# A two-layer encoder trunk in float32: the feed-forward's first projection by Strassen's seven products, tokens in two halves

## The chip, the cores and the metric

One Trainium2 chip, one core. The metric is the device time of one execution in microseconds (us), the median of several runs. The engines are named as the profile names them: PE (TensorE, matrix products), PEld (its weight loads), DVE (VectorE), ACT (ScalarE), POOL (GpSimd), SP (SyncE, which issues most DMA transfers). SBUF is the on-chip memory that all engines read, PSUM the banks that PE writes its sums to.

## What is computed

Two groups of tokens (272 and 1040 with the 16 meta tokens) pass through two layers of width 1024. Layer 0 mixes with a state-space scan and a gated recurrence, layer 1 with windowed attention; after each mixer comes the same gated feed-forward, on which the change works:

```python
def conv_ffn(h, w_up, conv_w, conv_b, w_down):      # w_up 1024 x 5632, w_down 2816 x 1024
    u = dwconv(h @ w_up, conv_w, conv_b, 1)          # width-3 depthwise convolution over tokens
    a, g = u[..., :2816], u[..., 2816:]
    return (gelu(g) * a) @ w_down

for layer in range(2):
    h = h + mixer(rmsnorm(h, norm_mix_g[layer]))
    h = h + conv_ffn(rmsnorm(h, norm_ffn_g[layer]), w_up[layer], ...)
h = rmsnorm(h, final_norm_g)
```

All of it is float32. PE multiplies in the format float32r; a product of two float32 matrices is made of three passes over a high part (the rounded value) and a low part (the rest): high x high, high x low, low x high.

## The kernel before, in words

Activations lie feature-major: 1024 features are 8 blocks of 128 partitions, and the 1316 columns are the tokens with pads. `hh` and `hl` (8 x 1316) hold the high and low parts of the normalized activations, `h` the residual, all in SBUF through the whole feed-forward.

`unit` (L233 to L243) brings in a weight unit of 128 x 1024 floats: a DMA on SP's queue, the high part by a cast on ACT (L241), the low part by a subtraction on DVE (L242), or on POOL where the caller asks for it, which only attention's projections do. `mm3_steps` (L251 to L261) issues the three passes: L256, L257 and L261.

`ffn` (from L320) takes the 22 blocks of 128 features of each half of `w_up` two at a time. For each block and each of three chunks of 438 tokens (440 columns with the neighbours that the convolution needs) `conv` makes 8 x 3 = 24 matmuls into one PSUM bank (tags a and b in turn), and the convolution on ACT (L337) and DVE (L339, L341), both straight out of PSUM. `gate` adds the gelu (ACT L347), the product with a (DVE L348), and the split into high and low parts (ACT L351, DVE L352). Then the two blocks of `w_down` are multiplied, chunk by chunk, 8 output blocks of 6 matmuls, into banks c and d, and DVE adds each to `h` (L384):

```python
for f in fs:
    ua = up_unit(f)
    a = [conv(f, c, *ua, "a") for c in range(NCH)]
    ug = up_unit(NF + f)
    for c in range(NCH):
        acts[f, c] = gate(f, c, a[c], ug)
downs = [self.unit(wd[f * 128:(f + 1) * 128, :], b=1024) for f in fs]
for c in range(NCH):
    for m in range(KD):
        ps = self.bank("cd")
        self.mm3(ps[:, :CH], [(downs[j][0][:, m * 128:(m + 1) * 128], ...) for j, f in enumerate(fs)])
        nc.vector.tensor_tensor(out=hs, in0=hs, in1=ps[:, :CH], op=ALU.add)
```

Per layer that is 44 x 3 x 24 = 3168 matmuls of 440 columns for the first projection and 11 x 3 x 8 x 6 = 1584 of 438 columns for the second. The weights are read once per layer.

`project_out` (L1247 to L1292) multiplies a mixer's output by its 1024 x 1024 matrix in three thirds of the tokens, 192 matmuls of about 438 columns each; in layer 1 the first third is done beside attention (`out_block`, L1202). `norm` (L265) makes the RMSNorm in four steps that are placed between other work. A scheduler orders the instructions of each engine by a simulation of its own; only in attention does the program's order stand for PE.

## Time and profile before

| | us |
|---|---|
| median of 3 runs (3090.25 to 3095.92) | 3090.98 |
| span of the profiled execution | 3089.7 |
| PE busy | 2934.9 (95%) |
| DVE busy | 1854.6 (60%) |
| ACT busy | 1133.7 (37%) |
| POOL busy | 200.9 (7%) |
| feed-forward of layer 0, about | 620 to 1560 |
| attention, about | 1560 to 2050 |
| feed-forward of layer 1, about | 2080 to 3010 |

The profiled execution's own time is its span, 3089.7 us; the runs' median lies 1.3 us above it. Matmuls overlap in the records (one lasts longer than the distance to the next), so a rate is read from the starts, or from a stretch divided by its count. DVE's records overlap a little in the same way.

### The profile page before, as it was taken

What the parts mean: (1) busy time and instruction counts of PE and PEld (TensorE: products, weight loads), DVE (VectorE), ACT (ScalarE), POOL (GpSimd) and SP (SyncE); (2) the same over time, 40 slices, a digit from 0 to 9 for tenths busy, and PEclk for the clock granted to TensorE, in tenths of its full rate; (3) what the DMA queues carried; (4) which work ended last, traced back from release to release, by engine and by line L of the source; (5) the groups of instructions that cost most, each with busy time, mean ns of one, the idle gap of its engine ahead of it and who ended that gap; (6) DMA issues with size and microseconds to landing.
All of it is one profiled execution on the core that took longest, in us unless ns stands there. A gap on an engine that the chain in (4) does not pass through costs nothing.

```text
span 3089.7 us, 39910 instructions
## 1 busy us (share of the span) xinstructions
PE 2934.9 (95%) x15424; PEld 2695.8 (87%) x15424; DVE 1854.6 (60%) x3386; ACT 1133.7 (37%) x2038; POOL 200.9 (7%) x356
## 2 busy tenths in 40 slices
PE   6999667999999999999999999989999999999998
PEld 5988446999999999999988887779999999999997
DVE  8998685365545555545574777757555555545555
ACT  4445683342222222222243666634222222222222
POOL 1000000000000000000003334300000000000000
PEclk9999788999999999999999999999999999999999
DMA  5331432311111011111136667761111011111101
GB/s 145 83 93 53 109 109 93 101 41 42 41 35 36 27 41 41 41 35 41 35 109 157 140 137 167 172 187 52 55 35 36 28 40 41 41 35 41 35 28 76
DMA packets 276376, 220.55 MB, mean 71 GB/s; under 512 B 33403, under 2 KB 257627, under 8 KB 276187
## 3 DMA queue, kind: packets, MB, share of 16 engines
q1 hardware_dynamic: 233755, 169.89, 19.4%
q0 software_dynamic: 35280, 31.98, 5.2%
q10 hardware_dynamic: 7152, 16.13, 1.4%
q8 instruction: 122, 2.00, 0.3%
q14 instruction: 67, 0.55, 0.1%
HBM read 167.71 MB, written 48.14 MB: 70 GB/s over the span
## 4 chain that ended last, share of the span: by engine, by line
PE 80%; DVE 10%; DMA 3%; ACT 3%; issue 2%; SPq 1%; POOL 0%; DVEq 0%; POOLq 0%; ACTq 0%
PE ps_a L256 10%; PE ps_a L261 10%; PE ps_a L257 9%; PE ps_b L261 7%; PE ps_b L257 7%; PE ps_b L256 7%; PE ps_d L261 4%; PE ps_c L261 4%; PE ps_d L256 4%; PE ps_d L257 4%; PE ps_c L256 4%; PE ps_c L257 4%; DVE z L692 1%; PE ps_c L1056 1%; PE ps_d L1075 1%
## 5 line engine op out<-in xcount | busy, mean ns | idle before, releaser
L256 PE MATMUL ps_a<-hh,whi 128*128 128x440 f32 (+4 forms) x1824 | 659.2, 362 | 29.4 <-ACT hh L907 17.3
L257 PE MATMUL ps_a<-hl,whi 128*128 128x440 f32 (+4 forms) x1824 | 654.6, 359 | 1.0 <-DVE hl L908 0.5
L261 PE MATMUL ps_a<-hh,wlo 128*128 128x440 f32 (+4 forms) x1824 | 653.2, 358 | 0.3 <-DVE wlo L242 0.3
L257 PE MATMUL ps_b<-hl,whi 128*128 128x440 f32 (+2 forms) x1136 | 413.0, 364 | 0.0
L261 PE MATMUL ps_b<-hh,wlo 128*128 128x440 f32 (+2 forms) x1136 | 412.1, 363 | 0.0
L256 PE MATMUL ps_b<-hh,whi 128*128 128x440 f32 (+2 forms) x1136 | 412.0, 363 | 0.0
L256 PEld LDWEIGHTS ps_a<-hh,whi 128*128 128x128 f32 x1824 | 348.2, 191 | 53.6 <-ACT hh L907 18.2
L242 DVE TENSOR_TENSOR wlo<-raw,whi 128x1024 fp32r<-128x1024 f32 x176 | 213.4, 1222 | 255.3 <-ACT whi L241 204.0
L261 PEld LDWEIGHTS ps_a<-hh,wlo 128*128 128x128 f32 x1824 | 347.7, 191 | 20.8 <-issue 2.6
L241 ACT CAST whi<-raw 128x1024 fp32r<-128x1024 f32 x194 | 201.1, 1047 | 448.0 <-PE ps_d L257 198.9
L257 PEld LDWEIGHTS ps_a<-hl,whi 128*128 128x128 f32 x1824 | 347.8, 191 | 18.6 <-DVE hl L231 1.0
L384 DVE TENSOR_TENSOR h<-h,ps_c 128x438 f32<-128x438 f32 x264 | 161.0, 610 | 175.6 <-PE ps_c L261 175.4
L384 DVE TENSOR_TENSOR h<-h,ps_d 128x438 f32<-128x438 f32 x264 | 161.1, 610 | 111.6 <-PE ps_d L261 111.0
L256 PEld LDWEIGHTS ps_b<-hh,whi 128*128 128x128 f32 x1136 | 214.3, 189 | 14.3
L261 PEld LDWEIGHTS ps_b<-hh,wlo 128*128 128x128 f32 x1136 | 213.8, 188 | 14.0
L257 PEld LDWEIGHTS ps_b<-hl,whi 128*128 128x128 f32 x1136 | 213.7, 188 | 13.5
L337 ACT ACTIVATE a<-ps_a,cw 128x438 f32<-128x438 f32 x92 | 65.9, 716 | 378.8 <-PE ps_a L261 375.2
L256 PE MATMUL ps_d<-xh,whi 128*128 128x438 f32 x528 | 191.5, 363 | 0.0
L256 PE MATMUL ps_c<-xh,whi 128*128 128x438 f32 x528 | 191.4, 362 | 0.0
L257 PE MATMUL ps_c<-xl,whi 128*128 128x438 f32 x528 | 191.0, 362 | 0.0
L261 PE MATMUL ps_c<-xh,wlo 128*128 128x438 f32 x528 | 191.0, 362 | 0.0
L257 PE MATMUL ps_d<-xl,whi 128*128 128x438 f32 x528 | 190.9, 361 | 0.0
(403 smaller groups left out, 4766.6 us busy)
## 6 DMA issues: line engine op xcount, KB each, us to landing
raw<-in_w_up SPq DMA_DIRECT2D x88, 512.0 KB
raw<-in_w_down SPq DMA_DIRECT2D x44, 512.0 KB
qs<-st SPq DMA_DIRECT2D x48, 219.0 KB
q<-qs POOLq DMA_DIRECT2D x80, 128.0 KB, 3.5
raw<-in_w_o SPq DMA_DIRECT2D x20, 512.0 KB
raw<-in_w_out_ab SPq DMA_DIRECT2D x16, 512.0 KB
raw<-in_w_in_ab SPq DMA_DIRECT2D x12, 512.0 KB
raw<-in_w_qkv SPq DMA_DIRECT2D x12, 512.0 KB
```

Source lines behind the costliest of these rows:

```text
L241: nc.scalar.copy(hi, raw)
L242: (low or nc.vector).tensor_tensor(out=lo, in0=raw, in1=hi.bitcast(F32), op=ALU.subtract)
L256: yield nc.tensor.matmul(ps, ah, bh, start=(j == 0), stop=False)
L257: yield nc.tensor.matmul(ps, ah, bl, start=False, stop=False)
L261: yield nc.tensor.matmul(ps, al, bh, start=False, stop=(j == n - 1))
L337: nc.scalar.activation(out=t, in_=ps[:, 1:CH + 1], func=AF.Identity, scale=cw[:, 1, m:m + 1], bias=cw[:, 3, m:m + 1])
L384: nc.vector.tensor_tensor(out=hs, in0=hs, in1=ps[:, :CH], op=ALU.add)
L692: v.tensor_tensor_scan(out=f0[h, s0:s0 + 4 * NK][:, ::step], data0=fm[h, ::step], data1=f1[h, 1:1 + 4 * NK][:, ::step], initial=0.0, op0=A ...
L1056: nc.tensor.transpose(pt[:m, j, :n], s[:n, j, j0:j0 + m], self.ident[:n, :n])
L1075: nc.tensor.matmul(ov, vt, y[:m, :, :n], start=(x + i == 0), stop=(last and i == 1))
```

## The change

The first projection. Two blocks of output features (256 rows), the 1024 input features as two halves of 512, and two quarters of the tokens make a 2 x 2 by 2 x 2 block product: eight block products, which Strassen's algorithm (in Winograd's form) makes with seven. `pair` does them: each is 4 x 3 = 12 matmuls of 330 or 332 columns. Per layer there are 22 pairs for each half of the tokens, so 2 x 22 x 7 x 12 = 3696 matmuls.

What the seven products need is made by other engines. `part` forms four sums of weight blocks a pair (five in the first two pairs of a half), 128 x 512, on POOL. `supply` splits each product's weights (128 x 512) into high and low parts: the cast on ACT, the subtraction on POOL for five products of seven and on DVE for products 4 and 7. There are 8 such tiles in turn, and `supply` runs 8 products ahead. `inputs` forms the sums and the splits of the activations, once per half of the tokens, in the SBUF space that `hh` and `hl` had. The products come out in PSUM as partial sums: `follow` adds them on DVE into SBUF tiles, and three of the four convolutions of a pair now read SBUF instead of PSUM.

The tokens. Each half (two quarters of about 328 columns) goes through all of `w_up` and `w_down`, so the weights are read, cast and split twice per layer. The second projection has 2 x 11 x 2 x 8 x 6 = 2112 matmuls of about 328 columns a layer, in all four pairs of banks. The residual lies in DRAM (`hsp`) and comes into SBUF half by half, the normalized activations of the second half likewise (`ysp`). `down_units` splits the weights of the second projection: ACT and POOL, 128 x 1024.

The order. In the feed-forward the program's order now stands for PE. For each two blocks of 128 gated features (called a group here) it is: the pair for a, the second projection of the group before (96 matmuls), the pair for g. So the pair for g and the next group's pair for a follow each other without the second projection between them. The first two pairs of a half are taken together, product by product.

Beside it: `project_out` works in four quarters instead of three thirds, two of them beside attention in layer 1; the last norm and the outputs of the first half come in the second half's first pairs; the ring for DMA descriptors that POOL writes is set to 8192.

The core of the diff (`ffn`, with the old body left out):

```diff
+        def part(j, p):
+            (a11, a12), (a21, a22) = ((t[:, :512], t[:, 512:]) for t in raws[j])
+            at = sums.setdefault(j, {1: a11, 2: a12, 4: a22})
+            def add(out, a, b, op):
+                nc.gpsimd.tensor_tensor(out=out, in0=a, in1=b, op=op)
+                return out
+            two = turns(j)
+            if p == 6:
+                at[5] = add(new(j % 2 if two else 0), a21, a22, ALU.add)
+                at[6] = add(at[5] if two else new(1), at[5], a11, ALU.subtract)
+                if not two:
+                    at[7] = add(new(2), a11, a21, ALU.subtract)
...
+            elif p == 3:
+                at[3] = add(at[6], a12, at[6], ALU.subtract)
+            return at[p]
+        def supply(t):
...
+            w = ops[j, p] = self.wsp.tile([128, 2, 512], FR, tag=tag, name=tag)
+            nc.scalar.copy(w[:, 0], src)
+            (v if p in (4, 7) else nc.gpsimd).tensor_tensor(out=w[:, 1], in0=src, in1=w[:, 0].bitcast(F32), op=ALU.subtract)
+            if i == 6:
+                load_raw(j + 2)
+        def convolve(src, m, n, out):
+            nc.scalar.activation(out=out[:, :n], in_=src[:, 1:n + 1], func=AF.Identity,
+                                 scale=cw[:, 1, m:m + 1], bias=cw[:, 3, m:m + 1])
+            for j, x in ((0, 0), (2, 2)):
+                v.scalar_tensor_tensor(out=out[:, :n], in0=src[:, x:x + n], scalar=cw[:, j, m:m + 1], in1=out[:, :n],
+                                       op0=ALU.mult, op1=ALU.add)
+            bank = {1: "a", 2: "a", 6: "b", 7: "c", 4: "c", 5: "d", 3: "d"}
+            def product(i):
+                p = order(j)[i]              # SEVEN = (1, 6, 2, 7, 5, 4, 3)
+                b = bank[p]
+                opens = p in (1, 6, 7, 5)
+                if opens:
+                    ps[b] = self.bank(b)[:, :n]
+                w, x = ops.pop((j, p)), X[p]
+                for k in range(4):
+                    for y, (e, f) in enumerate(((0, 0), (0, 1), (1, 0))):
+                        nc.tensor.matmul(ps[b], w[:, e, k * 128:(k + 1) * 128], x[:, f, k, :n], ...)
+            def follow(i):
+                p = order(j)[i]
+                if p == 1:
+                    st["u"] = tile("u", 2)[:, :n]
+                    nc.scalar.copy(st["u"], ps["a"])
+                elif p == 6:
+                    v.tensor_tensor(out=st["u"], in0=st["u"], in1=ps["b"], op=ALU.add)
+                elif p == 2:
+                    out(0, 0, ps["a"])
+                elif p == 7:
+                    st["v"] = tile("t", 3)[:, :n]
+                    v.tensor_tensor(out=st["v"], in0=st["u"], in1=ps["c"], op=ALU.add)
+                elif p == 5:
+                    v.tensor_tensor(out=st["v"], in0=st["v"], in1=ps["d"], op=ALU.add)
+                    out(1, 1, st["v"])
+                elif p in (4, 3):
+                    t = tile("t", 3)[:, :n]
+                    v.tensor_tensor(out=t, in0=st["u"], in1=ps["c" if p == 4 else "d"], op=ALU.add)
+                    out(*((1, 0) if p == 4 else (0, 1)), t)
...
+            for f0 in range(2, NF, 2):
+                ja = j0 + f0
+                run_pair(ja, s, X, hold, behind)
+                down(f0 - 2, ca)
+                down(f0 - 2, cb)
+                down_units(f0)
+                run_pair(ja + 1, s, X, gate)
```

Products 4 and 3 are added by PE onto the banks c and d that still hold products 7 and 5, so PE can start them only when DVE has read those (L442, L444 below); product 2 is added onto bank a, behind ACT's copy of product 1 (L435).

How the order of DVE reads, first in the feed-forward before, where a group's convolutions, gates and additions to `h` follow each other and nearly all read a PSUM bank:

```order
L339 SCALAR_TENSOR_TENSOR g<-ps_b,cw_654,g 128x438
L341 SCALAR_TENSOR_TENSOR g<-ps_b,cw_654,g 128x438
L348 TENSOR_TENSOR g<-g,a 128x438
L339 SCALAR_TENSOR_TENSOR a<-ps_a,cw_654,a 128x438
L352 TENSOR_TENSOR xl<-g,xh 128x438
L341 SCALAR_TENSOR_TENSOR a<-ps_a,cw_654,a 128x438
```

There is one subtraction of weights of 1024 columns (L242) for every two blocks or so between them, and POOL has nothing in these stretches.

Then DVE after the change, from the read of product 5 of a pair for g (L444, bank d) to the sum of products 1 and 6 of the next pair for a (L437); `t` and `xa` are tiles in SBUF, L398 a half of a convolution, L362 a subtraction of weights:

```order
L444 TENSOR_TENSOR t<-t,ps_d 128x332
L362 TENSOR_TENSOR wlo<-raw,wlo 128x512
L476 TENSOR_TENSOR xa<-t,xa 128x328
L398 SCALAR_TENSOR_TENSOR t<-t,cw_655 128x330
L448 TENSOR_TENSOR t<-u,ps_c 128x332
L398 SCALAR_TENSOR_TENSOR t<-t,cw_655 128x330
L473 TENSOR_TENSOR t<-t,a 128x330
L398 SCALAR_TENSOR_TENSOR t<-t,cw_655 128x328 x2
L476 TENSOR_TENSOR xa<-t,xa 128x330
L448 TENSOR_TENSOR t<-u,ps_d 128x332
L473 TENSOR_TENSOR t<-t,a 128x328
L437 TENSOR_TENSOR u<-u,ps_b 128x332
```

Nine of these read two SBUF tiles, four a PSUM bank. On the same engine, what follows up to the read of product 7 of that pair for a (L442, bank c), for which PE's product 4 waits:

```order
L398 SCALAR_TENSOR_TENSOR t<-t,cw_655 128x330 x2
L476 TENSOR_TENSOR xa<-t,xa 128x328
L362 TENSOR_TENSOR whi<-s_13985,whi 128x512
L473 TENSOR_TENSOR t<-t,a 128x330
L398 SCALAR_TENSOR_TENSOR a<-ps_a,cw_655,a 128x328
L442 TENSOR_TENSOR t<-u,ps_c 128x332
```

Five more with two SBUF tiles now stand between PE's product 7 and the read that lets product 4 start, all of them work on the pair before.

POOL in the feed-forward, where it had nothing before; these rows are about half of a group (L335 sums, L362 low parts, L485 low parts of the second projection; s_... are the tiles of the sums):

```order
L335 TENSOR_TENSOR s_9139<-raw 128x512
L362 TENSOR_TENSOR wlo<-s_8855,wlo 128x512
L362 TENSOR_TENSOR whi<-raw,whi 128x512
L335 TENSOR_TENSOR s_9141<-s_9139,raw 128x512
L485 TENSOR_TENSOR dl<-rawd,dh 128x1024
L362 TENSOR_TENSOR wlo<-s_9141,wlo 128x512
L362 TENSOR_TENSOR whi<-raw,whi 128x512
L335 TENSOR_TENSOR s_9141<-raw,s_9141 128x512
```

A whole group has 18 rows of 512 columns and 2 of 1024, and each reads two SBUF tiles.

## Rows read from the trace of the kernel before

**Rows 1.** The page: part 1, busy us and share; part 4, the chain's shares.

```profile
PE 2934.9 (95%) x15424; PEld 2695.8 (87%) x15424; DVE 1854.6 (60%) x3386; ACT 1133.7 (37%) x2038; POOL 200.9 (7%) x356
...
PE 80%; DVE 10%; DMA 3%; ACT 3%; issue 2%; SPq 1%; POOL 0%; DVEq 0%; POOLq 0%; ACTq 0%
```

**Rows 2.** Windows: busy us and count by engine, PEclk, DMA share, GB/s.

```profile
core 0: us, PE busy (x) PEld busy (x) DVE busy (x) ACT busy (x) POOL busy (x), PEclk, DMA share, GB/s
1560.00:2050.00 490.00, 464.99 (x2696) 409.68 (x2695) 344.89 (x872) 284.20 (x717) 150.68 (x245) 0.98 0.66 157
620.00:1560.00 940.00, 940.00 (x4715) 883.71 (x4715) 492.36 (x744) 245.03 (x356) 1.01 (x1) 1.00 0.13 38
2080.00:3010.00 930.00, 930.00 (x4667) 875.05 (x4666) 496.82 (x753) 246.13 (x356) 2.25 (x2) 1.00 0.13 39
```

**Rows 3.** Timeline of PE: first and last of 22 back-to-back matmuls, then of 25.

```profile
60.53 0.29 PE L261 MATMUL ps_a<-hh,wlo 128*128 128x272 f32 x1
...
63.24 0.29 PE L261 MATMUL ps_a<-hh,wlo 128*128 128x272 f32 x1
...
73.00 0.32 PE L256 MATMUL ps_a<-hh,whi 128*128 128x344 f32 x1
...
76.80 0.32 PE L256 MATMUL ps_a<-hh,whi 128*128 128x344 f32 x1
```

**Rows 4.** POOL's groups by form: count, busy us and mean ns of one.

```profile
L242 POOL TENSOR_TENSOR wlo<-raw,whi 128x1024 fp32r<-128x1024 f32 x18 | 43.9, 2443 | 10.7 <-ACT whi L241 9.9 <-issue 0.7
```

**Rows 5.** DVE's groups by form, 328, 512 and 1312 columns.

```profile
L683 DVE TENSOR_TENSOR z<-ps_b,cs 128x328 f32<-128x328 f32 x32 | 15.0, 488 | 0.0
L685 DVE TENSOR_TENSOR z<-z 128x328 f32<-128x328 f32 x16 | 7.9, 493 | 0.2
L618 DVE TENSOR_TENSOR w<-B,PW 128x512 f32<-128x512 f32 x16 | 10.7, 688 | 5.3 <-PE ps_c L626 5.1
L881 DVE TENSOR_TENSOR g<-g,xc 128x1312 f32<-128x1312 f32 x8 | 12.2, 1521 | 6.8 <-ACT g L821 6.7
```

**Rows 6.** Timeline of DVE, two neighbours of a dense stretch.

```profile
1569.29 0.61 DVE L280 TENSOR_TENSOR acc<-acc,t 128x438 f32<-128x438 f32 x1
1569.81 0.60 DVE L384 TENSOR_TENSOR h<-h,ps_d 128x438 f32<-128x438 f32 x1
```

**Rows 7.** ACT's groups by form: casts of 1024 and 438 columns, a convolution's first step.

```profile
L241 ACT CAST whi<-raw 128x1024 fp32r<-128x1024 f32 x194 | 201.1, 1047 | 448.0 <-PE ps_d L257 198.9 <-PE ps_a L257 179.3 <-PE ps_b L257 40.8
L351 ACT CAST xh<-g 128x438 fp32r<-128x438 f32 x132 | 73.6, 557 | 79.2 <-DVE g L348 79.2
L337 ACT ACTIVATE a<-ps_a,cw 128x438 f32<-128x438 f32 x92 | 65.9, 716 | 378.8 <-PE ps_a L261 375.2
```

**Rows 8.** Timeline of DVE and POOL where layer 0 passes into attention.

```profile
1594.13 2.95 POOL L242 TENSOR_TENSOR wlo<-raw,whi 128x1024 fp32r<-128x1024 f32 x1 [0.51 <-ACT whi L241]
1594.19 0.67 DVE L307 SCALAR_TENSOR_TENSOR t<-h,vec,y 128x438 f32<-128x438 f32 x1
1594.78 0.60 DVE L384 TENSOR_TENSOR h<-h,ps_c 128x438 f32<-128x438 f32 x1
1595.30 2.25 DVE L307 SCALAR_TENSOR_TENSOR t<-h,vec,y 128x438 f32<-128x438 f32 x1
...
1597.05 2.71 POOL L242 TENSOR_TENSOR wlo<-raw,whi 128x1024 fp32r<-128x1024 f32 x1
1597.47 2.75 DVE L307 SCALAR_TENSOR_TENSOR t<-h,vec,y 128x438 f32<-128x438 f32 x1
```

**Rows 9.** The same two engines in attention, two places.

```profile
1887.49 2.42 POOL L242 TENSOR_TENSOR wlo<-raw,whi 128x1024 fp32r<-128x1024 f32 x1
...
1888.57 0.67 DVE L1060 TENSOR_TENSOR tl<-ps_c,th 128x512 fp32r<-128x512 f32 x1
...
1898.27 2.37 POOL L242 TENSOR_TENSOR wlo<-raw,whi 128x1024 fp32r<-128x1024 f32 x1
1898.64 2.20 DVE L1239 TENSOR_TENSOR t<-t,y 128x165 f32<-128x165 f32 x1 [2.25 <-DMA y<-rs]
```

More of the change, by code (lines that the diff above doesn't have):

```diff
@@ L127, in setup @@
         self.hsp = self.dram.tile([128, KD, W], F32, tag="hsp", name="hsp")
+        self.ysp = self.dram.tile([128, KD, W - HALF], F32, tag="ysp", name="ysp")
     def small_vectors(self):
@@ new lines, in ffn @@
+        p_factors, p_spread, p_apply = p_norm
+        last = l == 1
+        up = [x + y for x in range(0, NF, 2) for y in (0, NF)]
+        seq = [m for _ in range(2) for m in up]
+        raws, sums, ops = {}, {}, {}
+        turns = lambda j: j % len(up) < 2
+        order = lambda j: TURNS if turns(j) else SEVEN
+        need = []
+        for j in range(0, len(seq), 2):
+            need += [(j + x, i) for i in range(7) for x in range(2)] if turns(j) else [(j + x, i) for x in range(2) for i in range(7)]
@@ new lines, in xtile, with inputs, new @@
+        def xtile():
+            return xs.tile([128, 2, 4, 332], FR, tag="x", name="x")
+        def inputs(first, ya, yb, n):
+            b11, b21, b12, b22 = ya[:, 0:4], ya[:, 4:8], yb[:, 0:4], yb[:, 4:8]
+            X = {1: first}
+            t = xtile()
+            u, w = (t[:, x, :, :n].bitcast(F32) for x in range(2))
+            def new(p, src):
+                X[p] = xtile()
+                self.split(X[p], src, n)
+            new(2, b21)
+            v.tensor_tensor(out=u, in0=b22, in1=b12, op=ALU.subtract)
+            v.tensor_tensor(out=w, in0=u, in1=b11, op=ALU.add)
+            new(6, w)
+            new(7, u)
+            nc.gpsimd.tensor_tensor(out=w, in0=b21, in1=w, op=ALU.subtract)
+            nc.gpsimd.tensor_tensor(out=u, in0=b12, in1=b11, op=ALU.subtract)
+            new(3, b22)
+            new(5, u)
+            new(4, w)
+            return X
@@ new lines, in step, with run_pair, hold, gate @@
+        def step(product, j, i):
+            product(i)
+            supply(need.index((j, i)) + 8)
+        def run_pair(j, s, X, sink, between={}):
+            product, follow = pair(j, s, X, sink)
+            for i in range(7):
+                step(product, j, i)
+                follow(i)
+                for f in between.get(i, ()):
+                    f()
+        held, acts, units = {}, {}, {}
+        def hold(x, q, t, n):
+            held[x, q] = t
+        def gate(x, q, g, n):
+            nc.scalar.activation(out=g[:, :n], in_=g[:, :n], func=AF.Gelu_apprx_tanh)
+            v.tensor_tensor(out=g[:, :n], in0=g[:, :n], in1=held[x, q][:, :n], op=ALU.mult)
+            xh, xl = (ap.tile([128, 332], FR, tag=f"{e}{x}{q}", name="xa")[:, :n] for e in "hl")
+            nc.scalar.copy(xh, g[:, :n])
+            v.tensor_tensor(out=xl, in0=g[:, :n], in1=xh.bitcast(F32), op=ALU.subtract)
+            acts[x, q] = xh, xl
@@ new lines, in project_out @@
+                    if l == 0:
+                        nc.scalar.copy(h, ps[:, :n])
+                    else:
+                        v.tensor_tensor(out=h, in0=h, in1=ps[:, :n], op=ALU.add)
+                    for f, x in behind.get(c, {}).get(j, ()):
+                        f(x)
+                if l == 0 and c == 1:
+                    v.tensor_copy(hb[:, :, 0:3], ha[:, :, HALF:HALF + 3])
+        square(3)
+        self.y = ha[:, :, QW[0][0]:QW[0][0] + QW[0][1]], ha[:, :, QW[1][0]:QW[1][0] + QW[1][1]]
```

524 lines of the change are left out of this document (306 added, 218 removed).

## The prediction

> **What bounds the kernel now.** I read the page first: PE is busy 95% of the span and carries 80% of the chain that ended last; POOL has 7% [rows 1]. Then the windows, because an average hides stages. In both feed-forward stretches PE is busy without a gap at full clock: 4715 recorded matmuls in 940 us and 4667 in 930 us, 0.1994 us each, with DMA at 13% and POOL at nothing; PE's idle time lies elsewhere, 25 us of it around attention [rows 2]. So in the stretches that the change rewrites, a saved matmul column is saved time, as long as the other engines keep up. The timeline tells what a narrower matmul costs: 272 columns follow each other every 2.71 / 21 = 0.1290 us, 344 columns every 3.80 / 24 = 0.1583 us [rows 3]. That is 0.407 ns a column and some 18 ns besides; it gives 0.1530 us for 331 columns (the mean of 330 and 332) and 0.1520 us for 328.
>
> **What PE gains.** First projection: 2 x 3168 = 6336 matmuls at 0.1994 = 1263 us become 2 x 3696 = 7392 at 0.1530 = 1131 us, 132 us less (a seventh product in eight, less the fixed part of more matmuls). Second projection: 3168 at 0.1994 = 632 us become 4224 at 0.1520 = 642 us, 10 us more. `project_out` in quarters: 1152 at 0.1994 = 230 us become 1536 at 0.1520 = 233 us, 3.5 us more. Together 118 us less.
>
> By the Trainium skill's page TensorE: Matmul & The Clock Gate (Back-to-back issue gap) a warm matmul costs its columns at 2.4 GHz and 2.5 ns. With that an estimate of the saving is 136 us and the whole would come out 18 us lower; the 344 columns above take 0.1583 us where it gives 0.146, so the rows decide.
>
> **What the other engines must do for it.** A group (two blocks, one half of the tokens) takes PE 2 x 84 x 0.1530 = 25.7 us for the pairs and 96 x 0.1520 = 14.6 us for the second projection, 40.3 us; there are 44 groups. ACT has 14 casts of 512 columns (half of 1.047 us), 2 of 1024, and 18 instructions of about 330 columns at three quarters of 0.557 to 0.716 us [rows 7]: 18 us, which fits. DMA brings 6 loads of 512 KB a group, 3.1 MB in 40.3 us, 78 GB/s; the attention stretch moved 157 GB/s on average [rows 2], so reading the weights twice costs nothing by bandwidth. The cover is the 8 tiles of lead, 14.7 us of products; where it is gone (the one buffer for `w_down`'s second block) ACT's cast waits with the gelu queued behind it.
>
> POOL is another matter. One subtraction of 1024 columns took it 2.44 us [rows 4]; half of that, 1.22 us, I take for 512. A group has 18 such and 2 long ones: 27 us, within 40.3. DVE has 50 instructions of about 330 columns and 4 of 512. By its rows 328 columns last 0.49 us and 512 columns 0.69 [rows 5]; in a dense stretch the next starts 0.09 us before the record ends [rows 6], so 0.40 and 0.60 in sequence: 22 us, within 40.3 too.
>
> By the Trainium skill's page GPSIMD Engine Reference (Performance versus the Vector engine) a POOL addition of 2048 columns takes 4497 ns. From that and the row an estimate for 512 is 1.42 us instead of 1.22, which would add 1.8 us to the stall below in each group, some 70 us in all. No row has 512 columns on POOL.
>
> **Where they collide.** The two engines cannot both be at work on it. At 1594.13 POOL starts a subtraction; a DVE instruction with two inputs in SBUF, issued at 1595.30, lasts 2.25 us in place of 0.67 and ends 0.47 us after POOL's, and the next one again, 2.75 us [rows 8]. In between POOL's two also take 2.95 and 2.71 us in place of 2.44: they alternate, each blocked for the whole of the other. In attention an instruction of 165 columns needs 2.20 us for the same reason, while one that reads PSUM beside the same POOL work takes its usual 0.67 [rows 9]. Before, this hardly mattered: POOL did 18 subtractions in the whole run [rows 4]. Now 24 of DVE's 54 instructions in a group read two SBUF tiles (12 halves of convolutions, 8 of the gate, 4 low parts), and all 24 are made while the two neighbouring pairs run, none for the second projection.
>
> The tight place is the one of the order above. When product 5 of the pair for g ends, PE goes on through seven products (4, 3, and then 1, 6, 2, 7, 5 of the pair for a), 7 x 12 x 0.1530 = 12.9 us, before product 4, which waits for DVE's read of bank c. DVE has to do 14 instructions with two SBUF inputs by then (12 x 0.40 + 2 x 0.60 = 6.0 us) and six with PSUM (2.4 us): 8.4 us, and alone it would be 4.5 us early. But in these 12.9 us PE also frees seven operand tiles, and POOL has 9 instructions for every seven: 11.0 us. On the port that both need that is 6.0 + 11.0 = 17.0 us in 12.9 us. I take the difference, **4.1 us of PE stall a group**. ACT's copy of product 1, behind which product 2 waits, stands behind a cast of DVE's results and will be late in the same way. The bounds: nothing, if POOL falls behind there and catches up in the 14.6 us of the second projection, where the port is free; and 14 x 1.22 - 4.5 = 12.6 us, if every one of the fourteen waits for a whole POOL instruction. I take the sum between them: the rows are nearest to strict alternation, which keeps POOL from falling far behind, and POOL can do no more than the freed tiles ask for. There are 10 such places in each half of the tokens, 40 in all: 40 x 4.1 = 164 us.
>
> **The starts of the halves.** `inputs` is 8 DVE instructions of 1328 columns at 1.5 us [rows 5] and 2 on POOL, most with two SBUF inputs, 12 us that come on top in the first 25.7 us of pairs; in the second half they also wait for `ysp` from DRAM, and stand in DVE's queue ahead of the gate's work. Nothing to 20 us each; I take 7, four times 28 us.
>
> **Taken as nothing.** Attention takes one more block of output projection beside its tiles, and has 25 us of PE idle to hold it [rows 2]; the norms lie between products as before; the last outputs come after a quarter instead of a third. Each is worth a few us either way, inside the range. PE stalls of 2 us may cost clock: where PE was 95% busy the granted clock was 0.98 [rows 2], 1 or 2% of the feed-forward at worst, 40 us.
>
> **The sum**, against the profiled execution: 3089.7 - 118 + 164 + 28 = 3163.7 us, and 1.3 us more for the runs' median: **3165 us**, 2.4% slower. The change trades a PE that never waited for one that does 6% less work and waits 10% of a group.
>
> **The rivals.**
> - *The port is shared out well* (faster). POOL's work slips into the second projection's 14.6 us and into DVE's own waits, and the stall is 0 to 2 us a group. For it: over a whole group the port is asked for 27 + 24 x 0.40 + 0.8 = 37 us of 40.3, so there is room in the sum, and eight tiles of lead allow the slip. Against it: the alternation of the rows, under which DVE cannot go first. The time: 3091 - 118 + 28 + 40 x (0 to 2) = 3001 to 3081 us. The point from which it decides is (118 - 28) / 40 = 2.2 us a group: below that the change is faster. Chance 0.39.
> - *The port governs everything*: 6 us or more a group, with the clock at 0.98. For it: ACT's queue stands in order behind DVE, and 512 columns on POOL may cost more than half of 1024. Against it: POOL runs out of work while PE stands still. 3091 - 118 + 28 + 40 x 6 + 40 = 3281 us. Chance 0.11.
> - *The loads govern*: two readings of the weights come late. Against it: 78 of at least 157 GB/s. It would add some 3 us a group, as my forecast does, at another wait. Chance 0.03.
> - That the change does not do what it says is excluded by the order: PE's rows fall into seven products a pair.
>
> **How the numbers follow.** My forecast, a stall of 2.2 to 6 us a group, has 0.47 and alone would reach from 3089 to 3255 us. The first rival's 0.39 lies below 3081, the other two above or within. A measurement can tell 0.2%, 6 us, from no change; the strip from 3085 to 3097 holds some 0.04 between the cases. So faster 0.39, same 0.04, slower 0.57. The range runs from 3010, leaving the best tenth, to 3265.
>
> **What would show it.** Right: POOL busy 1400 us or more and DVE's two-input instructions of 330 columns at a mean of 0.8 us or more instead of 0.49; in a group's window PE busy below 90%, with waits for DVE (reads of c and d) and for ACT's copy of product 1; matmuls of 330 columns 0.153 us apart where they run. Wrong: those DVE instructions at 0.5 us, or PE without gaps in the pairs; then the time is near 3010. If PE waits mainly for weights, the loads or POOL's own rate were the bound and not the port.

## The result: 3564 us, 15% slower

| | us |
|---|---|
| before, median of 4 runs (3089.3 to 3095.9) | 3090.6 |
| the change, median of 4 runs (3559.5 to 3568.4) | 3564.1 |
| ratio, 95% interval | 1.1537 (1.1517 to 1.1556) |
| forecast and range | 3165 (3010 to 3265) |
| span of the profiled execution | 3566.6 |

The sign and the mechanism were as forecast, the size was not: 474 us more instead of 74. The page of the change, parts 1 and 4, against [rows 1]:

```profile
PE 2937.0 (82%) x17944; PEld 2790.8 (78%) x17944; DVE 2700.5 (76%) x4391; ACT 1518.6 (43%) x2921; POOL 1614.5 (45%) x1270
...
PE 45%; DVE 29%; issue 10%; DMA 6%; ACT 6%; POOL 3%; SPq 0%; DVEq 0%; ACTq 0%; POOLq 0%
```

PE is as long busy as before although it has 4% less to do (the forecast's 118 us of 2935), and its idle time grew from 155 to 630 us; its mean granted clock fell from 0.976 to 0.922. DVE's busy time grew by 846 us and its part of the chain from 10% to 29%. The windows say where, and at what clock (columns as in [rows 2]):

```profile
core 0: us, PE busy (x) PEld busy (x) DVE busy (x) ACT busy (x) POOL busy (x), PEclk, DMA share, GB/s
900.00:1100.00 200.00, 173.01 (x1070) 169.79 (x1069) 158.19 (x219) 75.15 (x136) 120.61 (x80) 0.95 0.21 64
1200.00:1300.00 100.00, 66.77 (x419) 65.15 (x419) 85.67 (x105) 46.00 (x78) 59.53 (x32) 0.85 0.38 121
640.00:760.00 120.00, 77.50 (x434) 75.06 (x433) 94.46 (x105) 42.24 (x71) 78.92 (x47) 0.79 0.40 125
...
926.20:928.40 2.20, 2.13 (x14) 2.13 (x15) 2.20 (x2) 0.50 (x2) 2.19 (x2) 1.00 0.00 0
936.30:940.20 3.90, 3.80 (x14) 3.80 (x15) 3.90 (x6) 1.35 (x4) 3.82 (x3) 0.50 0.43 123
940.20:944.00 3.80, 3.80 (x21) 3.80 (x21) 3.80 (x7) 2.35 (x4) 1.75 (x3) 0.75 0.55 156
```

The first row is the steady stretch of groups: PE 86.5% busy at a granted clock of 0.95. The next two are a change of halves and the start of layer 0's feed-forward, where PE is busy two thirds of the time. The last three are short stretches of the group shown below. PE's waits (in total, how many, the longest), the first five and three further down:

```profile
PE ps_c L427 <- DVE t L442: 152.3, 38, 5.7
PE ps_a L427 <- ACT u L435: 64.0, 41, 6.0
PE ps_a L248 <- ACT xa L475: 54.4, 4, 21.0
PE ps_d L427 <- DVE t L444: 41.8, 37, 1.6
PE ps_a L248 <- DVE hr L1436: 30.4, 1, 30.4
...
PE ps_a L427 <- POOL wlo L362: 19.4, 2, 10.4
PE ps_a L427 <- ACT wlo L361: 18.7, 2, 12.1
...
PE ps_a L252 <- DMA xr<-in_x_sample: 12.6, 2, 11.9
```

Three of them come once a group: product 4 waits for DVE's read of bank c (L442), product 2 for ACT's copy of product 1 (L435), product 3 for the read of bank d (L444). Four of the 41 waits for L435, 17.8 us, lie at starts of halves; the other lines belong to the starts and to the work outside the feed-forward (`hr` is the block of the residual that a block of output projection is added to, `xr` a tile of the tokens' rows). The groups by form, of POOL and DVE, against [rows 4] and [rows 5]:

```profile
L485 POOL TENSOR_TENSOR dl<-rawd,dh 128x1024 fp32r<-128x1024 f32 x88 | 213.5, 2426 | 479.7 <-ACT dh L484 479.7
L362 POOL TENSOR_TENSOR whi<-s,whi 128x512 fp32r<-128x512 f32 x132 | 201.2, 1525 | 62.6 <-ACT whi L361 62.6
...
L398 DVE SCALAR_TENSOR_TENSOR t<-t,cw 128x328 f32<-128x328 f32 x176 | 195.6, 1111 | 6.3 <-ACT t L395 2.1
L473 DVE TENSOR_TENSOR t<-t,a 128x328 f32<-128x328 f32 x132 | 160.0, 1212 | 33.7 <-ACT t L472 33.3
...
L495 DVE TENSOR_TENSOR hs<-hs,ps_d 128x328 f32<-128x328 f32 x132 | 65.0, 492 | 32.8 <-PE ps_d L253 32.6
```

DVE's instructions of 328 columns with two SBUF inputs take 1.04 to 1.21 us by group instead of 0.49 (the halves of a convolution from PSUM take 0.55); those that add from PSUM still take 0.49. One group, in its timeline:

```profile
916.04 2.40 POOL L485 TENSOR_TENSOR dl<-rawd,dh 128x1024 fp32r<-128x1024 f32 x1
...
916.13 2.01 PE L427 MATMUL ps_c<-x,whi 128*128 128x330 f32 x12
...
916.60 2.20 DVE L473 TENSOR_TENSOR t<-t,a 128x328 f32<-128x328 f32 x1 [0.55 <-ACT t L472]
...
918.72 0.49 DVE L444 TENSOR_TENSOR t<-t,ps_d 128x330 f32<-128x330 f32 x1
...
919.26 2.08 PE L427 MATMUL ps_d<-x,wlo 128*128 128x330 f32 x12 [1.12 <-DVE t L444]
...
923.99 0.48 ACT L472 ACTIVATE t<-t 128x328 f32<-128x328 f32 x1 [3.52 <-DVE t L398]
...
925.80 0.42 ACT L435 COPY u<-ps_a 128x330 f32<-128x330 f32 x1
...
926.27 2.08 PE L427 MATMUL ps_a<-x,whi 128*128 128x330 f32 x12 [1.24 <-ACT u L435]
...
935.86 0.48 DVE L442 TENSOR_TENSOR t<-u,ps_c 128x330 f32<-128x330 f32 x1
...
936.40 3.67 PE L427 MATMUL ps_c<-x,wlo 128*128 128x330 f32 x12 [4.40 <-DVE t L442]
939.87 3.00 PE L427 MATMUL ps_d<-x,whi 128*128 128x330 f32 x12
```

From the read of bank d (918.72) to that of bank c (935.86) DVE needs 17.1 us, and product 4 then waits 4.40 us where the forecast had 4.1. But the forecast's 17.0 us of work on the port are counted from the end of product 5, when PE goes on (916.13), and from there DVE needs 19.7 us. The 2.6 us between are in the main the product with a (L473), which POOL's long subtraction (L485) holds for 2.20 us and for which PE waits 1.12 us. Not priced in the forecast are this wait, the 1.24 us at ACT's copy (L435), in whose queue a gelu (L472) stood 3.52 us for DVE, and the clock: after the 4.40 us wait two products start 3.47 and 2.83 us before the next, instead of 1.83, with the granted clock at 0.50 (1.2 GHz) until some time in the second of them; after the 1.24 us it stays at 1.00.

This group lies in a first half. There the wait for bank c is 4.4 us in nearly every group, in the second halves 3.6 (5.7 in the last one). Over the 36 such waits of 3.5 us or more, the two products behind lose 1.4 to 2.8 us, 2.0 on average; the group shown is one of the dearer ones.

Between the first long subtraction (L485) of one group and that of the next lie 49.2 us on average (36 intervals, in four stretches of ten groups). PE needs 40.3. So **a group loses 8.9 us, of which the forecast had 4.1**.

### The profile page after: what moved, and what is told of

Read it like the earlier page. It is cut to its first block, busy times and chain, and to the rows that moved or that the text cites. A ratio compares the mean times of both kernels' runs of the same rounds, so it can differ in the third digit from the quotient of the medians.

```text
span 3566.6 us, 48939 instructions
## 1 busy us (share of the span) xinstructions
PE 2937.0 (82%) x17944; PEld 2790.8 (78%) x17944; DVE 2700.5 (76%) x4391; ACT 1518.6 (43%) x2921; POOL 1614.5 (45%) x1270
## 4 chain that ended last, share of the span: by engine, by line
PE 45%; DVE 29%; issue 10%; DMA 6%; ACT 6%; POOL 3%; SPq 0%; DVEq 0%; ACTq 0%; POOLq 0%
DVE t L398 7%; PE ps_a L427 4%; PE ps_c L427 4%; PE ps_a L253 4%; PE ps_a L248 4%; PE ps_a L249 4%; PE ps_d L427 3%; DVE wlo L362 2%; DVE xa L476 2%; PE ps_b L427 2%; PE ps_c L248 2%; PE ps_c L253 2%; PE ps_c L249 2%; PE ps_b L253 2%; PE ps_b L248 2%
## 5 line engine op out<-in xcount | busy, mean ns | idle before, releaser
L485 POOL TENSOR_TENSOR dl<-rawd,dh 128x1024 fp32r<-128x1024 f32 x88 | 213.5, 2426 | 479.7 <-ACT dh L484 479.7
L427 PE MATMUL ps_c<-x,wlo 128*128 128x332 f32 (+1 forms) x1056 | 234.6, 386 | 150.3 <-DVE t L442 150.3
L248 PE MATMUL ps_a<-hh,whi 128*128 128x438 f32 (+5 forms) x848 | 294.9, 348 | 66.3 <-DVE hr L1436 30.4
L427 PEld LDWEIGHTS ps_c<-x,wlo 128*128 128x128 f32 x1056 | 214.3, 246 | 160.6 <-DVE t L442 160.6
L335 POOL TENSOR_TENSOR s<-raw 128x512 f32<-128x512 f32 x184 | 277.4, 1509 | 92.7 <-DVE whi L362 38.0
L398 DVE SCALAR_TENSOR_TENSOR t<-t,cw 128x328 f32<-128x328 f32 (+1 forms) x264 | 304.4, 1153 | 7.6 <-ACT t L395 2.6
L249 PE MATMUL ps_a<-hl,whi 128*128 128x438 f32 (+5 forms) x848 | 289.9, 342 | 1.0 <-DVE hl L598 0.4
L253 PE MATMUL ps_a<-hh,wlo 128*128 128x438 f32 (+5 forms) x848 | 289.1, 341 | 0.0
L398 DVE SCALAR_TENSOR_TENSOR a<-t,cw,a 128x328 f32<-128x328 f32 (+1 forms) x264 | 277.2, 1061 | 6.1 <-ACT a L395 5.6
L362 POOL TENSOR_TENSOR whi<-s,whi 128x512 fp32r<-128x512 f32 x132 | 201.2, 1525 | 62.6 <-ACT whi L361 62.6
L473 DVE TENSOR_TENSOR t<-t,a 128x328 f32<-128x328 f32 (+1 forms) x176 | 184.8, 1050 | 44.7 <-ACT t L472 44.2
L427 PE MATMUL ps_d<-x,wlo 128*128 128x332 f32 (+1 forms) x1056 | 179.2, 318 | 43.0 <-DVE t L444 41.8
L362 POOL TENSOR_TENSOR wlo<-s,wlo 128x512 fp32r<-128x512 f32 x132 | 192.2, 1457 | 31.4 <-ACT wlo L361 31.3
```

Of the source, the lines that this page charges most:

```text
L248: yield nc.tensor.matmul(ps, ah, bh, start=(j == 0), stop=False)
L249: yield nc.tensor.matmul(ps, ah, bl, start=False, stop=False)
L253: yield nc.tensor.matmul(ps, al, bh, start=False, stop=(j == n - 1))
L335: nc.gpsimd.tensor_tensor(out=out, in0=a, in1=b, op=op)
L362: (v if p in (4, 7) else nc.gpsimd).tensor_tensor(out=w[:, 1], in0=src, in1=w[:, 0].bitcast(F32), op=ALU.subtract)
L398: v.scalar_tensor_tensor(out=out[:, :n], in0=src[:, x:x + n], scalar=cw[:, j, m:m + 1], in1=out[:, :n], op0=ALU.mult, op1=ALU.add)
```

## The experiments

By *port* the prediction and this text mean a way to SBUF that an instruction of DVE with two SBUF inputs and one of POOL cannot use at the same time; what the traces show of it is that the two hold each other up, as in [rows 8] and above. The theory: the port makes DVE late. The rival: DVE is late by its own number and order of instructions. All ratios are to the kernel before, run beside each. The edits shift line numbers: the change's L473 is L463 in e1_pool_idle and L474 in e3_conv_psum and e5_no_two_sbuf.

| run | us | ratio (95%) |
|---|---|---|
| e1_pool_idle | 3128.9 | 1.012 (1.010 to 1.014) |
| e2_all_dve | 3449.5 | 1.116 (1.114 to 1.118) |
| e3_conv_psum | 3341.2 | 1.081 (1.079 to 1.083) |
| e5_no_two_sbuf | 3186.4 | 1.031 (1.029 to 1.033) |
| g1_dl_dve | 3511.4 | 1.137 (1.135 to 1.139) |
| f1_late_inputs | 3182.4 | 1.029 (1.028 to 1.031) |
| f2_start_dve | 3187.0 | 1.031 (1.030 to 1.033) |
| f3_attention | 3162.8 | 1.023 (1.022 to 1.025) |
| f4_all | 3165.3 | 1.024 (1.022 to 1.026) |
| f6_starts | 3161.6 | 1.023 (1.022 to 1.025) |
| f8_early | 3168.8 | 1.025 (1.023 to 1.027) |
| h1_no_splits | 3127.7 | 1.012 (1.011 to 1.014) |
| h2_no_pool_start | 3131.7 | 1.014 (1.012 to 1.015) |
| h3_neither | 3110.9 | 1.007 (1.005 to 1.009) |

### The port, or DVE itself

**POOL idle.**

```diff
-            (v if p in (4, 7) else nc.gpsimd).tensor_tensor(out=w[:, 1], ...)
+            if p in (4, 7):
+                v.tensor_tensor(out=w[:, 1], ...)
...
-                nc.gpsimd.tensor_tensor(out=lo, in0=raw, ...)
-                units[f0 + x] = hi, lo
+                units[f0 + x] = hi, hi
...
-            if p == 6: ...
+            at.update({3: a12, 5: a21, 6: a11, 7: a21})
```

> All of POOL's work in the feed-forward's groups is left out: the sums of weight blocks are not formed (a plain block stands in for each), and the low parts that POOL made are not made (the high part is multiplied a second time in their place, for the first projection and the second). Matmuls, DVE's and ACT's instructions keep their number and size; the output is not the reference's. The port (my theory): DVE's instructions with two SBUF inputs of about 330 columns fall from 1.05 to 1.15 us back to about 0.49, PE's waits for L442, L444 and ACT's copy of product 1 fall below 1 us a group, a group takes 41 to 42 us instead of 49, the granted clock in a group is 1.0, and the time is 3010 to 3130 us. Rival, DVE's own number of instructions and their order: the same 54 instructions stand in the same queue, product 4 waits as before, a group stays at 46 us or more and the time above 3400 us.

Measured 3128.9 us. The steady window of this kernel, and one of DVE's groups by form:

```profile
900.00:1100.00 200.00, 200.00 (x1318) 200.00 (x1318) 133.67 (x271) 94.33 (x171) 0.00 (x0) 1.00 0.27 80
```
```profile
L463 DVE TENSOR_TENSOR t<-t,a 128x328 f32<-128x328 f32 x132 | 65.8, 499 | 55.8 <-ACT t L462 55.2
```

With the same matmuls and the same DVE and ACT instructions PE has no gap, at full clock, 0.1517 us a matmul; a group of 264 takes 40.06 us. DVE's instructions with two SBUF inputs are back at 0.50 to 0.62 us. DVE's order alone stalls nothing: the rival falls.

**The same work, all on DVE.**

```diff
-                nc.gpsimd.tensor_tensor(out=out, in0=a, in1=b, op=op)
+                v.tensor_tensor(out=out, in0=a, in1=b, op=op)
...
-            (v if p in (4, 7) else nc.gpsimd).tensor_tensor(out=w[:, 1], ...)
+            v.tensor_tensor(out=w[:, 1], ...)
...
-                nc.gpsimd.tensor_tensor(out=lo, in0=raw, ...)
+                v.tensor_tensor(out=lo, in0=raw, ...)
```

> All 20 instructions that POOL has in a group go to DVE: same computation, POOL idle. The port: DVE gets 18 x 0.60 + 2 x 1.2 = 13 us more in a group, 22 + 13 = 35 us of 40.3, but none of its instructions waits for POOL; a group takes 41 to 45 us, the time is 3080 to 3250 us, far below 3564. Rival, DVE's load and order: DVE is the engine that is late, and with 37% more instructions it is later still: above 3564 us.

Measured 3449.5 us: faster than the change, as the theory has it, but 200 us above its range. DVE's instructions last what they last alone, and yet, in the timeline of DVE and PE:

```profile
989.66 0.49 DVE L444 TENSOR_TENSOR t<-t,ps_d 128x330 f32<-128x330 f32 x1
990.07 0.68 DVE L335 TENSOR_TENSOR s<-raw 128x512 f32<-128x512 f32 x1
...
1005.34 0.50 DVE L442 TENSOR_TENSOR t<-u,ps_c 128x330 f32<-128x330 f32 x1
...
1005.89 3.67 PE L427 MATMUL ps_c<-x,wlo 128*128 128x330 f32 x12 [4.41 <-DVE t L442]
```

From L444 to L442 DVE works without a pause for 15.7 us, with eleven of POOL's former instructions in it, and product 4 waits 4.41 us, as long as in the group of the change. A group takes 47.6 us where I expected 41 to 45. My expectation averaged 35 us over a group of 40.3; the place between the two reads decides. There DVE alone needs 15.7 us for about what it and POOL together needed 17.1 us for: sharing the work over the port bought nothing in this place. So DVE's own load, the rival, is a limit too when all of this work is DVE's. Of PE's three waits only those for L435 and L444 are nearly gone (18.9 and 5.5 us).

**Fewer instructions on the port.** The sums of products stay in PSUM, and the convolutions read them there:

```diff
-                    v.tensor_tensor(out=st["v"], in0=st["v"], in1=ps["d"], op=ALU.add)
-                    out(1, 1, st["v"])
+                    t = st["v"] if turns(j) else ps["b"]
+                    v.tensor_tensor(out=t, in0=st["v"], in1=ps["d"], op=ALU.add)
+                    out(1, 1, t)
...
-                    t = tile("t", 3)[:, :n]
-                    v.tensor_tensor(out=t, in0=st["u"], in1=ps["c" if p == 4 else "d"], op=ALU.add)
+                    t = ps["c" if p == 4 else "d"]
+                    v.tensor_tensor(out=t, in0=st["u"], in1=t, op=ALU.add)
```

> The sums of products (L444, L448) are written to the PSUM banks b, c and d instead of SBUF tiles, so that all four convolutions of a pair read PSUM: 12 of the 24 DVE instructions with two SBUF inputs in a group become ones with one, their number stays, POOL's work stays. The port: these 12 fall from 1.1 to about 0.49 us, some 7 us of DVE time a group; a group falls from 49 to 41 to 44 us, and the time to 3150 to 3330 us. Rival, DVE's number of instructions and their order: nothing changes by more than 1%, 3530 to 3600 us.

Measured 3341.2 us, 11 us above the range of the port and far outside the rival's. The groups by form of this kernel:

```profile
L474 DVE TENSOR_TENSOR t<-t,a 128x328 f32<-128x328 f32 x132 | 184.3, 1397 | 23.0 <-ACT t L473 22.9
...
L477 DVE TENSOR_TENSOR xa<-t,xa 128x328 fp32r<-128x328 f32 x132 | 103.4, 784 | 4.7 <-ACT xa L476 2.3
...
L398 DVE SCALAR_TENSOR_TENSOR t<-ps_c,cw,t 128x328 f32<-128x328 f32 x88 | 48.2, 548 | 0.4 <-ACT t L395 0.3
```

The number of instructions and POOL's work are unchanged; the moved ones fall to 0.55 us. Of those left on the port the split (L477) falls to 0.78 us and the product with a (L474) rises to 1.40. PE's wait for L442 falls from 4.0 to 1.7 us each, that for bank d stays at 1.1.

**None on the port.** In addition to the edit of e3_conv_psum, the gelu's output goes to the PSUM bank of its block (g, handed on by `out`), and all seven low parts to POOL:

```diff
-        def gate(x, q, g, n):
-            nc.scalar.activation(out=g[:, :n], in_=g[:, :n], func=AF.Gelu_apprx_tanh)
+        def gate(x, q, t, n, g):
+            nc.scalar.activation(out=g[:, :n], in_=t[:, :n], func=AF.Gelu_apprx_tanh)
...
-            (v if p in (4, 7) else nc.gpsimd).tensor_tensor(out=w[:, 1], ...)
+            nc.gpsimd.tensor_tensor(out=w[:, 1], ...)
```

> As e3_conv_psum, and besides the gelu is written to the PSUM bank of its block, so that the product with a and the split read one PSUM and one SBUF operand, and the 4 low parts of a group that DVE made go to POOL. No DVE instruction of a group has two SBUF inputs; POOL has 22 of 512 columns and 2 of 1024, 22 x 1.30 + 2 x 2.43 = 33.5 us of 40.3. The port: POOL's instructions take 1.30 us, DVE's 0.4 to 0.5, a group 40.5 to 43 us, the clock is 1.0, the time 3010 to 3130 us. Rival, POOL's own load: operand tiles come late, PE waits for L362 and a group takes 44 us or more: above 3200 us. Rival, DVE's order: above 3400 us.

Measured 3186.4 us, 378 us less than the change. Its steady window, and one of POOL's and one of DVE's groups by form:

```profile
900.00:1100.00 200.00, 200.00 (x1318) 200.00 (x1318) 119.31 (x250) 94.29 (x170) 162.17 (x121) 1.00 0.26 79
```
```profile
L335 POOL TENSOR_TENSOR s<-raw 128x512 f32<-128x512 f32 x184 | 248.1, 1350 | 20.0 <-PE ps_d L253 14.8 <-DMA raw<-in_w_up 4.4
...
L474 DVE TENSOR_TENSOR ps_a<-ps_a,a 128x328 f32<-128x328 f32 x44 | 22.3, 508 | 29.8 <-ACT ps_a L473 29.8
```

POOL has more to do than in the change (81% of this window against 60%) and PE never waits. The port is the cause of the groups' loss, and 40.06 us a group is all that PE asks. The time is still 56 us above the expected range: since PE has no gap in the steady groups, the rest lies outside them.

**One wait alone.** An edit of the change itself, in `down_units`:

```diff
-                nc.gpsimd.tensor_tensor(out=lo, in0=raw, ...)
+                v.tensor_tensor(out=lo, in0=raw, ...)
```

> The changed kernel (3564 us) with one edit: the two low parts of 1024 columns a group, which POOL makes in 2.4 us each and which hold up DVE's product with a (L473) for 2.2 us ahead of the read of product 5, go to DVE. The port: PE's wait for L444 (41.8 us over 37 places) falls below 10 us and the time by 45 to 90 us, to 3475 to 3520 us; the wait for L442 stays at 4 us or more a group, since neither long one lies in that place. Rival (DVE's load): two more instructions of 1.2 us a group on the late engine, 3564 us or more.

Measured 3511.4 us, 53 us less. The wait for L444 is no longer among PE's longest waits, whose first two are now:

```profile
PE ps_c L427 <- DVE t L442: 176.1, 40, 5.7
PE ps_a L427 <- ACT u L435: 48.8, 23, 7.7
```

The wait for L442 stays, 4.4 us each instead of 4.0, and 5.6 in the first halves: part of what PE no longer waits for bank d and the copy it now waits at bank c, to which it comes earlier. Time and waits came out as expected, so the reading of the timeline holds.

### Starts of halves, and what is outside the feed-forward

From the traces, the two feed-forwards together (first matmul of the first projection to the last addition to `hs`), less 44 groups of 40.3 us; the rest of the span is outside:

| | feed-forward | above 1773 | outside |
|---|---|---|---|
| before, about | 1916 | - | 1174 |
| the change | 2336 | 563 | 1230 |
| e1_pool_idle | 1905 | 132 | 1226 |
| e5_no_two_sbuf | 1951 | 178 | 1234 |
| f3_attention | 1970 | 197 | 1193 |
| h1_no_splits | 1934 | 161 | 1190 |
| h2_no_pool_start | 1930 | 157 | 1200 |
| h3_neither | 1910 | 137 | 1202 |

Of the change's 563 us, 40 x 8.9 = 356 lie in the groups; 207 are left for the four starts, 52 us each, the ends of the halves included. The feed-forwards before had 1916 - 9504 x 0.1994 = 21 us above their matmuls. Where a group takes 40.06 us, as in e1, the third column is some 10 us too low: 141 us for the starts of e1, and 147 for those of h3. The runs that follow build on e5_no_two_sbuf; f4_all has the edits of f1, f2 and f3 together.

```diff
# f1_late_inputs
                 yb = xtile().rearrange("p a k n -> p (a k) n").bitcast(F32)
+                v.tensor_copy(yb[:, 0, 0:1], acts[1, 1][1][:, 0:1].bitcast(F32))
                 self.dma(yb, self.ysp[:, :, 328:660])
# f2_start_dve
-            nc.gpsimd.tensor_tensor(out=w, in0=b21, in1=w, op=ALU.subtract)
+            v.tensor_tensor(out=w, in0=b21, in1=w, op=ALU.subtract)
...
+            (v if turns(j) and j % 2 else nc.gpsimd).tensor_tensor(out=w[:, 1], ...)
# f3_attention
-            rows(99)
             for _ in fill:
                 pass
+            rows(99)
...
-                            xr = p.tile([128, D], F32, tag="xr", name="xr")
+                            xr = p.tile([128, D], F32, tag="xr", name="xr", bufs=6)
```

> e5_no_two_sbuf (3186 us), with one column written into the tile of ysp's second quarter from the last gate's result before it is loaded, so that the sums and splits of the second half's activations come behind the gate on DVE and ACT. Queue theory (at a change of halves PE stands 14 us because three splits of 1328 columns, 2.9 us each beside POOL, stand ahead of the last gate on DVE): two changes, 10 to 14 us each, 3158 to 3168 us. Rival (the stall only moves: the splits are needed for product 6 of the next half soon after): within 6 us of 3186.

> e5_no_two_sbuf with the two sums of activations in inputs on DVE instead of POOL, and in the first two pairs of a half the low parts of every second pair on DVE. POOL theory (the first pairs of a layer ask POOL for 2.4 us a product while PE takes 1.84, and the two sums of 3 to 4 us stand between): POOL is relieved by 7 x 1.3 + 7 = 16 us at each of four starts; 10 us gained at the start of a layer and 5 at a change of halves, 3150 to 3170 us. Rival (the port again: DVE's new instructions with two SBUF inputs are blocked by POOL's and block them): 3180 us or more.

> e5_no_two_sbuf with two edits outside the feed-forward: behind attention's last tile, the loads that stage the last rows are issued behind those of the remaining output blocks instead of ahead of them, and the tokens' rows for project_out have six buffers instead of four. Queue theory (PE's 28 us wait for the addition to hr is a load that stands behind others on SP's queue; its 12 us wait for xr is a missing buffer): 15 to 28 us and 10 us less, 3146 to 3162 us. Rival (the chain of loads through DRAM only ends later, and project_out waits for it instead): only the 10 us, 3174 to 3180 us.

> All edits of f1, f2 and f3 together. If their gains add: 3186 less 25, 25 and 32 = 3104 us (3085 to 3135), 0.5% above the kernel before. If they share one limit (the splits of activations, or POOL): 3135 us or more.

f1 gained 4 us, which is within the scatter of the runs (3181 to 3192 for e5, 3179 to 3184 for f1), and f2 nothing: both rivals hold. f3 gained 24, 1 us short of the range of its theory; its two waits are gone: outside the feed-forward the span fell by 41 us, and 19 of them came back as later starts. f4, all three, is no better than f3. In f4 the wait for the gate at the first change of halves is down to 4.6 us, and in its place stand the norm's column sums, late on the same DVE:

```profile
PE ps_c L279 <- DVE acc L272: 14.3, 1, 14.3
PE ps_c L292 <- DVE t L289: 9.8, 1, 9.8
PE ps_a L248 <- ACT xa L476: 4.6, 1, 4.6
```

f6 starts from f3 with the edit of f1; it moves these sums into the next pair and, as f8 alone on f3, opens the pools of the second pair's raw weights and of the weight sums ahead of `project_out` in layer 1.

```diff
# f6_starts; the last three lines also f8_early
-            acc = st[c] = tile("acc", n)
+            acc = st[c] = tile("acc", n, 2)
...
-                    behind = {1: [lambda: hfactors(1)], ...}
+                    behind = {0: [lambda: hfactors(0)], 1: [lambda: hfactors(1)], ...}
...
-                down(end, cb, {} if last else {4: [lambda: hfactors(0)]})
+                down(end, cb)
...
+                    if l == 1:
+                        self.wr = right.enter_context(tc.tile_pool(name="wr", bufs=2, side=RIGHT))
+                        self.ss = right.enter_context(tc.tile_pool(name="ss", bufs=1, side=RIGHT))
```

> f3_attention (3163 us; five buffers for the tokens' rows instead of six) with three edits at the starts of halves: the second half's activations come behind the last gate (as in f1_late_inputs); the norm's column sums of the first finished quarter, which PE then waited 14 us for (its wait for DVE's acc in f4_all), are multiplied in the next pair instead of inside the last second projection; and in layer 1 the raw weights and weight sums of the first pairs get space of their own instead of the space that project_out holds until its last matmul. Memory theory (a start costs 35 to 70 us because nothing of it can begin before the old tiles are free, and the norm and the splits queue there): 10 to 15 us at each change of halves and 10 to 20 at layer 1's start, 3110 to 3135 us. Rival (the work of a start, 7 splits, 4 sums and 8 operand tiles, is itself longer than what PE has for it): less than 12 us, 3150 us or more.

> f3_attention with the last edit of f6_starts alone: in layer 1 the raw weights of the second pair and the weight sums have space of their own, so that they are loaded and formed before project_out's last matmul. Memory theory: PE's waits for L362 and L361 at layer 1's start (some 23 us in f4_all) fall by 10 to 20 us, 3143 to 3153 us. Rival (the activations' splits end last there): within 5 us of 3163.

Neither gained; f8 came out 6 us above f3. In f6 the first change of halves has no wait above 3.6 us any more, but five buffers for xr bring 11.5 us of waiting back, and layer 1's start waits 22.3 us for the column sums (11.9 in f3) instead of for its weights. So each edit at a start moved a wait to the next late thing. What the work of a start is worth is shown by leaving it out:

```diff
# h1_no_splits, in inputs
-            t = xtile()
...
+            for p, src in ((2, b21), (6, b22), (7, b12), (3, b22), (5, b12), (4, b21)):
+                X[p] = xtile()
+                nc.scalar.copy(X[p][:, 0, :, :n], src)
...
+                        nc.tensor.matmul(ps[b], w[...], x[:, f if p == 1 else 0, k, :n], ...)
# h2_no_pool_start, in part, supply and product
+            if two:
+                at.update({3: a12, 5: a21, 6: a11, 7: a21})
...
+            if not turns(j):
+                nc.gpsimd.tensor_tensor(out=w[:, 1], ...)
...
+                        nc.tensor.matmul(ps[b], w[:, 0 if turns(j) else e, ...], x[...], ...)
```

> f3_attention (3163 us) with the activations' sums and low parts left out at every start of a half: inputs only casts six plain blocks, and the high part is multiplied in place of the low one (product 1 keeps its own); the output is not the reference's, the matmuls are as many. If a start waits for DVE's 12 instructions of 1328 columns: 15 to 25 us at each of four starts, 3065 to 3105 us. If it waits for POOL's sums and low parts of the first two pairs: less than 20 us in all, 3143 us or more.

> f3_attention with POOL's sums and low parts left out in the first two pairs of each half alone (a plain block stands in for a sum, the high part for the low one); the output is not the reference's, the matmuls are as many. If a start waits for POOL: 15 to 25 us at each of four, 3065 to 3105 us. If it waits for DVE's splits: less than 20 us in all, 3143 us or more.

> Both omissions of h1_no_splits and h2_no_pool_start. If the two hinder each other on the port, or the one takes the other's place as the limit, this gains more than either: 25 to 40 us a start, 3005 to 3065 us, below the kernel before; what is then left above the 1773 us that PE needs in the feed-forward is due to loads, the norm and the last gate. If a third cause rules the starts (loads, the norm's column sums, the last gate): 3130 us or more.

Against f3 they gained 35, 31 and 52 us (34, 30 and 51 by the ratios): 9, 8 and 13 us a start, between the expected cases each time. (What h1 leaves out is 8 instructions of DVE and 2 of POOL a start, not the 12 of its expectation.) Neither DVE's splits nor POOL's supply is the limit alone, and with both gone the feed-forward is still 137 us above what PE needs. PE's waits of h3 in the first 120 us of layer 0's feed-forward:

```profile
PE ps_a L416 <- ACT wlo L363: 8.4, 1, 8.4
PE ps_a L248 <- ACT dh L474: 5.0, 1, 5.0
PE ps_a L253 <- POOL dl L475: 4.1, 2, 2.1
```

The cast of the second pair's first weights, then the cast and the split of the first `w_down` blocks. How this remainder divides among loads, memory that comes free late, the norm and the clock was not settled.

No run beat the kernel before; the best without an omission, f6_starts and f3_attention, are alike and 2.3% slower than it.

## Why the prediction was wrong, step by step

**Right.** The matmuls: 0.1517 us apart where the forecast had 0.1520 and 0.1530. The mechanism: 1614 us of POOL (1400 or more foretold), DVE's two-input instructions at 1.1 us (0.8 or more), waits for reads of c and d and for the copy of product 1. The wait for bank c: 4.0 us on average (4.4 and 3.6 in the two halves) against 4.1. That it fits so well is in part luck. The forecast's sum begins at the end of product 5; from there DVE took 19.7 us and not 17.0, and PE waited three times, 1.12 + 1.24 + 4.40 = 6.8 us. In the sum POOL's instructions of 512 columns stood at 1.22 us (1.32 to 1.56 measured), and its long one was missing. DMA was no bound: 64 GB/s in the groups, and e1 and e5 run them without a gap at 80 and 79.

**Wrong by size.** The profiled execution came out 403 us above the sum of 3163.7. Three terms of "the sum" account for it:

- *The stall of 4.1 us a group, 40 times.* It is 8.9: 40 x (8.9 - 4.1) = 192 us. I priced one wait of three. ACT's copy of product 1 I named as "late in the same way" and gave it nothing (1.2 to 1.3 us a group, 46 of the 64.0 us in the run); the read of bank d (1.1 to 1.2 us a group, 41.8 us) I did not see, because I counted POOL's work by a mean and left its long instructions out of the place (g1: 53 us). And the clock, "1 or 2% of the feed-forward at worst, 40 us", stood in the range and not in the sum: the products behind the waits for bank c lose 2.0 us on average, 72 us over 36 places. The three waits and the clock make 8.4 of the 8.9 us.
- *The starts, four times 7 us.* Some 160 us more than the 28: 207 us, less the 28 and less the 21 that the feed-forwards before already had. POOL's work makes a third of the 207: in e1 the starts cost 141. The rest is a chain in which DVE, ACT, POOL and loads each come last in turn (f1 to h3). I took DVE's time for the splits as the price; the price is what PE waits until the first tiles, sums, splits, column sums and weights are all there.
- *Taken as nothing: attention and the rest.* 56 us, where I had 3.5. 12 us are a missing buffer for xr; 30 us are the wait for `hr`, which f3 took away by issuing the staging loads later (the two shares are read from PE's waits; f3 took both away in one run, 41 us). I had set the block of output projection against 25 us of idle PE and not asked what is queued ahead of its load on SP's queue.

The rival "the port governs everything" (3281 us, 6 us or more a group) was the right case, with a chance of 0.11, and even it left the starts at 7 us each and had the clock at 0.98, where the groups show 0.95. What I held against it, "POOL runs out of work while PE stands still", bounds the one place that I had summed; the other two waits and the clock came on top of it. The upper end of 3255 us for a stall of 6 us does not follow from the terms, which give 3091 - 118 + 28 + 40 x 6 = 3241; the measured time lies far above both.

The Trainium skill's page SBUF — State Buffer (Who interferes with whom) says that a DVE instruction with two SBUF inputs and a POOL instruction that reads SBUF exclude each other for a whole instruction, and that one with at most one SBUF input does not contend outside what the page calls 2-port modes. The traces agree: a product with a of 2.20 us behind a subtraction of 2.40, and 0.51 us beside a busier POOL once the other input is in PSUM (e5).

## What to carry to other kernels

Add up the work of all engines that share a port in the place between two reads that PE waits for, not over a whole round: DVE with some 35 us of work for 40.3 still stalls PE by 4.4 us in each round (e2). If DVE and POOL must both work, give DVE's instructions one operand in PSUM; that, with DVE's four low parts a group moved to POOL, took back 378 us of 474 here, with POOL busier than before. And a new start or change of phase has a price of its own (some 35 us with most of its work left out, 52 in the change, four times; the kernel before had two, some 10 us each) that a saving of matmuls must first pay: by the forecast's count the two projections saved some 30 us for each half of the tokens in a layer ((118 + 3.5) / 4).

## What was not expected of the hardware

- POOL's instruction of 512 columns takes 1.32 to 1.35 us by group where no DVE instruction of a group has two SBUF inputs (e5), more than half of the 2.42 us for 1024; the forecast took 1.22. The forecast's estimate by the Trainium skill's page GPSIMD Engine Reference (Performance versus the Vector engine) and the row of 1024 columns was 1.42.
- The cost of the port is not shared evenly: beside POOL, DVE's instructions of 328 columns went from 0.50 to 0.62 us by group (e1) to 1.04 to 1.21, POOL's of 512 columns from 1.32 to 1.35 (e5) to 1.32 to 1.56.
- In the group shown PE's granted clock stayed at 1.00 after a wait of 1.24 us and was at 0.50 after one of 4.40 us; such a wait of 3.6 to 4.4 us, once in every group, cost another 2.0 us on average.
